# Four sample blocks at a time, the last product in two PSUM tiles, and a redrawn order of steps

## Chip, core and metric

The kernel runs on one core of a Trainium2 chip. The metric is the device time of one execution in microseconds (us). Engines are called as in the profile: PE (TensorE, matmuls; PEld its weight loads), DVE (VectorE), ACT (ScalarE), POOL (GpSimd), SP (SyncE, which here issues most DMA transfers).

## What is computed

The reference is one step of a decoder layer with D_MODEL 1024, for a prompt of 1024 tokens and a sample of 8 tokens. The parts that matter here are the last two:

```python
m = (jax.nn.sigmoid(g_a) * jnp.einsum('ble,ed->bld', y_a, w_pa)
     + jax.nn.sigmoid(g_b) * jnp.einsum('ble,ed->bld', y_b, w_pb))
h = h + _rmsnorm(jnp.einsum('bld,de->ble', m, w_out), post_g)
e = jnp.einsum('blp,pd->bld', p, w_ple)
gate = jax.nn.sigmoid(jnp.einsum('bld,de->ble', _rmsnorm(h, ple_in_g), w_pg))
h = h + _rmsnorm(gate * e, ple_out_g)
```

The product with `w_out` is called "output" below and the product with `w_pg` "gate". Ahead of them lie the combined input projection with its seven branches, the spatial gating, the pooling, and the products with `w_pa` and `w_pb`. All data are float32; products are formed from a high and a low part of each operand (three matmuls, high x high, high x low, low x high).

## The kernel before

**Products.** Each 1024 x 1024 product is made in four "pairs" of 256 rows or tokens, and each pair by Strassen's scheme: seven products P1 to P7 of half size in place of eight. One such product is one *step*: it prepares its weights, runs 12 matmuls of up to 512 columns into a PSUM tile, and has the tile evacuated by ACT or DVE. In output and gate the tokens are the stationary operand (`Turned`) and the rows are tokens (`Tokens`); PSUM tiles called `acct` come from three buffers. Output pairs 1 to 3 and all gate pairs go through `strassen_within` (line 757), whose tile `r2` takes P6, P5 and P3 one after the other by accumulation, with reads in between. In the trace the operand's name tells the product: `woB11`/`wgB11` is P1, `T2` P6, `T3` P7, `T1` P5, `B21` P2, `B22` P3, `T4` P4; a final h or l is the high or low part.

**The last gate pair** uses the order `LAST` (P1, P6, P7, P5, P2, P4, P3). Its last product, P3, is made in two column halves of 256 (`run_halves`, line 791), both in the one tile `r2`, and each half is handed to `user.direct`, which for the gate is `gated` (line 1586): a sigmoid on ACT out of PSUM, a product with the embedding on DVE, a sum of squares on ACT and a product with the gain on DVE. `gate_finish` then takes the root on POOL and writes the last rows of the result.

**The sample** (8 tokens) takes its output and gate rows from `sample_steps` (line 934). For both, eight blocks of 128 rows of the weights (`worow`, `wgrow`, 512 KB each) are loaded, and a *round* (`sample_round`, line 903) multiplies two blocks by the sample's 8 columns in four float32 matmuls that use four column groups of the array at once and accumulate in four parts of one bank, `sps`. Rounds are put between the steps of the prompt's products: loads after steps 0, 2, 4, 6 and rounds after steps 2, 4, 6, 8, counted from `OS` in output and `GS` in gate (line 36). After the last round `sample_sums` adds the four parts; output's sample then goes through `out_finish(S)` (norm, and a transfer on POOL's queue that adds `x_sample` to `hs`), `gate_norm(S)` and `gate_input(S)`.

**The order of the work** is not that of the source. A planner (`Planner`, line 95) collects all operations with estimated durations (`duration`), due times (`late`, worked back from PE's uses) and landing times of transfers (`lands`), then lets a simulated machine choose, on each engine, among what is ready. `LOAD` and `LEAD` say how long before its due time an operation may start, `PATIENCE` how long it may be passed over, and `HASTE` is the patience of the steps in `TURNS`. `TURNS` says after which step of output and gate (seven steps per pair, 0 to 27 output, 28 to 55 gate) the finish, the gate's norm and the turning of h for the gate are recorded for each pair of token blocks. The engines then run these orders as they stand, each in its own order. All operations are issued by one line, 369, which is why the profile names that line everywhere.

Of the kernel before, what the change touches and what calls it, by code (L numbers as in the profile page):

```python
# [11 lines left out]
AF = mybir.ActivationFunctionType  # L12
# [4 lines left out]
NB = D // P  # L17
# [3 lines left out]
HALF = 512  # L21
QUART = 256
# [2 lines left out]
QT = WIDE // 2  # L25
EPS = 1e-6
POOL_BUF = 15
FAST = (1, 1, 0, 1)
SIDES = (0, 1, 0, 1, 0, 0, 0, 0)
EARLY = 40.0  # L30
WE = 2
PUSH = {'norm': -5.0, 'half': 0.0, 'cut': 0.0, 'e': -4.0, 'we': -4.0, 'vw': -5.0, 'p': -1.0}
WARM = 8
HASTE = 8.0
TURNS = ((7, 8, 11), (14, 14, 18), (21, 26, 28), (30, 33, 35))
OS, GS = 5, 12
WINDOWS = (2, 4, 8, 16)
PLE = 256
SLOTS = 46
# [55 lines left out]
class Planner:  # L95
# [5 lines left out]

    SEEN = {"tensor": 0.25, "vector": 0.15, "scalar": 0.20, "gpsimd": 0.20}
    TABLES = {AF.Gelu_apprx_tanh: 1, AF.Sigmoid: 2, AF.Silu: 3}
    LOAD, LEAD, PATIENCE, RATE, SPARE = 14.98, 14.0, 55.8, 0.36, 3
    SPARED = 1.0

    def __init__(self, nc, slots, queues):
# [98 lines left out]
    def take(self, engine, method, args, kwargs):  # L206
        given = [*(("out" if i == 0 else "", a) for i, a in enumerate(args)), *kwargs.items()]
        writes = [a for k, a in given if k in ("out", "accum_out") and a is not None]
        reads = [a for k, a in given if k not in ("out", "accum_out") and hasattr(a, "tensor")]
        if kwargs.get("accum_op") is not None:  # L210
            reads += writes
        name = writes[0].tensor.name
        if engine == "tensor" and self.open is not None and self.open[0] == name:
            op = self.open[1]
        else:
            op = Op(engine, len(self.ops), self.clock, self.fixed)
            op.patience, op.push = self.patience, self.push
            self.ops.append(op)
        self.open = (name, op) if engine == "tensor" else None
        op.calls.append((method, args, kwargs))  # L220
        op.spent.append(op.busy)
        if method == "dma_start":
            run = min(self.run(a) for a in (writes[0], reads[0]))
            op.busy, op.moved = 1.0 if engine == "gpsimd" else 0.45, writes[0].size() * 4e-6 * (1 + 0.2 / run)
            op.lands = 2.0
            if kwargs.get("accum_op") is not None:
                op.moved, op.lands = 2 * op.moved, 3.5
        else:
            took = self.duration(engine, method, writes[0], reads, kwargs)
            op.busy += took  # L230
            if engine == "tensor" and not self.fixed:
                self.clock += took
            if engine == "scalar":
                op.table = self.TABLES.get(kwargs["func"], 0)
        for ap in reads:
            self.touch(op, ap, False)
        for ap in writes:
            self.touch(op, ap, True)
# [138 lines left out]
def hybrid_step(  # L377
# [7 lines left out]
    nc = tc.nc  # L385
# [6 lines left out]
    plan = Planner(nc, SLOTS, {"acc": 3, "bank": 2})  # L392
# [42 lines left out]
    def add(out, a, b):  # L435
        nc.vector.tensor_tensor(out=out, in0=a, in1=b, op=ALU.add)
# [17 lines left out]
    nc = plan  # L454
# [39 lines left out]
    class Operand:  # L494
# [37 lines left out]
        def at(self, what, k):  # L532
            return [part[:, k % 2, :] for part in self.parts[what, k // 2]]

    class Stored(Operand):


        ROWS = {"B11": ("b", 0, 0), "B21": ("b", 1, 0), "B22": ("b", 1, 1), "T2": ("low", 0, 0),
                "T1": ("low", 0, 1), "T4": ("high", 0, 0), "T3": ("high", 0, 1)}
# [71 lines left out]
    class Features:  # L611

        new = staticmethod(lambda: region("acc"))
# [16 lines left out]
    class Tokens:  # L630

        new = staticmethod(lambda: region("acct")[:, 0])
        view = staticmethod(lambda ps, wide: ps)
        pieces = staticmethod(lambda ps, wide: [(ps, slice(0, HALF))])
# [1 line left out]
        tail = False  # L636
        like = staticmethod(lambda t: t)

    def columns(c):

        class Part(Tokens):
            pieces = staticmethod(lambda ps, wide: [(ps[:, c], c)])
        return Part

    class Turned(Weights):

# [11 lines left out]
    def product(form, ps, weights, operand, what, first, last, again=False):  # L658

        plan.apart()  # L660
        wide = what not in ("B11", "B21", "T4")
        for k in range(4):
            if k == 2 and plan.clock < EARLY:
                plan.apart()
            (wh, wl), (xh, xl) = weights, operand.at(what, k)
            for i, (w, x) in enumerate(((wh, xh), (wh, xl), (wl, xh))):
                for o, c in form.pieces(ps, wide):
                    nc.tensor.matmul(o, w[:, k, :], x[:, c],
                                     start=first and k == 0 and i == 0, stop=last and k == 3 and i == 2,
                                     skip_group_check=again)  # L670
# [86 lines left out]
    def strassen_within(weights, operand, user, order=None):  # L757

        steps, at = [], {}
        plan = (("P1", "A11", "B11", "r1"), ("P6", "S2", "T2", "r2"), ("P7", "S3", "T3", "r3"),  # L760
                ("P5", "S1", "T1", "r2"), ("P2", "A12", "B21", "r1"), ("P3", "S4", "B22", "r2"),
                ("P4", "A22", "T4", "r3"))
        place = {p: r for p, _, _, r in plan}

        def evacuate(p):
            ps = at[place[p]]
            if p == "P1":
                both = slot("u", (P, 2, HALF))
                at["u"], at["w"] = both[:, 0], both[:, 1]
                nc.scalar.activation(out=at["w"], in_=ps, func=AF.Copy)  # L770
            elif p == "P6":
                add(ps, ps, at["w"])
                nc.scalar.activation(out=at["u"], in_=ps, func=AF.Copy)
            elif p == "P5":
                nc.scalar.activation(out=at["w"], in_=ps, func=AF.Copy)
                user.summed(1, 1, at["r3"], at["w"])
            elif p == "P2":
                user.direct(0, 0, ps)
            elif p == "P3":
                user.direct(0, 1, ps)  # L780
            elif p == "P4":
                user.summed(1, 0, ps, at["u"])

        for p, a, b, r in sorted(plan, key=lambda x: order.index(x[0])) if order else plan:
            def run(a=a, b=b, r=r):
                new = r not in at
                if new:
                    at[r] = Tokens.new()
                product(Tokens, at[r], weights.ready[a], operand, b, new, True, not new)

            def run_halves(a=a, b=b, r=r):
                for c in (slice(0, QUART), slice(QUART, HALF)):
                    product(columns(c), at[r], weights.ready[a], operand, b, False, True, True)
                    user.direct(0, 1, at[r][:, c], slice(HALF + c.start, HALF + c.stop))

            if order and p == order[-1]:
                steps.append(Step(lambda a=a: weights.prepare(a), run_halves, nothing))
            else:
                steps.append(Step(lambda a=a: weights.prepare(a), run, lambda p=p: evacuate(p)))
        steps[0].loads = lambda: (weights.fetch(), user.loads())  # L800
        steps[-1].after.append(user.finish)
        return steps

    class User:

        func = AF.Copy
# [93 lines left out]
                nc.tensor.matmul(ps, hi(k), wl, start=False, stop=False)  # L900
                nc.tensor.matmul(ps, lo(k), wh, start=False, stop=k == w.nk - 1)

    def sample_round(ps, turned, weights, r):

        plan.apart()
        for q in range(4):
            k, j = r + q // 2, q % 2
            nc.tensor.matmul(ps[32 * q : 32 * q + NS, :], turned[k], weights(k, j),
                             start=r == 0, stop=r == len(turned) - 2)
# [24 lines left out]
    def sample_steps(key, src, steps, turned, finish):  # L934
        rows, ps = {}, []

        def load(r):
            for k in (r, r + 1):
                t = rows[k] = slot(f"{key}row", (P, D))
                dma(t, src[k * P : (k + 1) * P, :])  # L940

        def run(r):
            if not ps:
                ps.append(bank("sps"))
            sample_round(ps[0], turned(), lambda k, j: rows[k][:, j * HALF : (j + 1) * HALF], r)
            if r == NB - 2:
                finish(ps[0])

        for i, r in enumerate(range(0, NB, 2)):
            at(steps[2 * i], lambda r=r: load(r))  # L950
            at(steps[2 * i + 2], lambda r=r: run(r))


    roots = {}
# [64 lines left out]
    turned = dram.tile([SEQ, D], F32, tag="vturned", name="vturned")  # L1019
# [9 lines left out]
    class V(User):  # L1029

        func = AF.Gelu_apprx_tanh
# [158 lines left out]
    class Gate(User):  # L1190
        func = AF.Sigmoid
# [7 lines left out]
    class U(User):  # L1199
        func = AF.Gelu_apprx_tanh  # L1200
# [4 lines left out]
    class ZA(User):  # L1205
        func = AF.Silu
# [84 lines left out]
    class ZB(User):  # L1291
        func = AF.Silu
# [102 lines left out]
    steps = [s for p in vsteps + gasteps for s in p] + every(usteps)  # L1395
# [8 lines left out]
    c = vsteps[0]  # L1404
# [471 lines left out]
```

## Time and profile before

| | us |
|---|---|
| median of 3 runs | 981.69 |
| the three runs | 981.69, 984.54, 978.53 |
| the profiled execution's own time | 979.92 |
| its span (first to last instruction) | 978.2 |
| PE busy in the span | 965.4 |
| DVE busy | 805.7 |
| ACT busy | 495.5 |

The profile belongs to one execution, and durations read from it are compared with that execution's own time; what lies between its span and its time (1.72 us) is before the first and after the last instruction. In a row of the timeline the columns are start and duration in us, engine, line, operation, output <- input, shapes, and count; a bracket at the end tells how long the engine had idled and what ended the idling. A row of the waits has total us, number of waits and the longest. A row of the table by stretches has the length, then busy time and instructions of PE, PEld, DVE, ACT and POOL (or of the one engine that was asked for), the granted clock of PE, the share of the DMA engines and GB/s.

### The profile page before, as it was taken

To read this page: it belongs to the slowest core of one execution; us is meant where nothing else is said; L and a number is where in the kernel's file an instruction comes from. 1 tells how busy PE (TensorE), PEld (TensorE's weight loads), DVE (VectorE), ACT (ScalarE), POOL (GpSimd) and SP (SyncE) were. 2 spreads that over 40 slices of the span, in tenths; PEclk is the share of its full clock that TensorE was granted. 3 is DMA by queue.
4 is the path that set the end of the run, shared out by engine and by line. 5 is a ranking of instruction groups with operands and counts; after the bars stand their busy time and mean duration, and the time that the engine had idled before them with its cause. 6 is when DMAs were issued, how large, how long until landed. Compare 5 with 4: busy or idle time off the path is not lost. (4 is left out here: it accounts for less than half of the span.)

```text
span 978.2 us, 15914 instructions
## 1 busy us (share of the span) xinstructions
PE 965.4 (99%) x6048; PEld 858.1 (88%) x6048; DVE 805.7 (82%) x1251; ACT 495.5 (51%) x847; POOL 72.8 (7%) x117
## 2 busy tenths in 40 slices
PE   9999999999999999999999999999999999999996
PEld 7889999999999998999999999999999997778775
DVE  7798568978879789887777897698699899779987
ACT  7674346767434544242423343463363273688655
POOL 2200000000000000000010100000000001323212
PEclk9999999999999999999999999999999999999998
DMA  9464654423457787541222266692592385698996
GB/s 347 148 151 88 152 135 148 162 95 116 171 213 275 257 281 238 188 153 54 87 76 93 75 218 244 222 376 91 170 370 87 120 306 177 160 300 296 222 326 209
DMA packets 128505, 185.81 MB, mean 190 GB/s; under 512 B 42150, under 2 KB 85198, under 8 KB 128421
## 3 DMA queue, kind: packets, MB, share of 16 engines
q1 hardware_dynamic: 126093, 176.91, 54.4%
q0 software_dynamic: 2048, 7.37, 4.2%
q8 instruction: 47, 0.77, 0.3%
q10 hardware_dynamic: 288, 0.52, 0.2%
q14 instruction: 29, 0.24, 0.1%
HBM read 129.27 MB, written 55.96 MB: 189 GB/s over the span
## 5 line engine op out<-in xcount | busy, mean ns | idle before, releaser
L369 DVE TENSOR_TENSOR u<-acc,u 128x520 f32<-128x520 f32 (+1 forms) x90 | 62.5, 695 | 29.8 <-PE acc L369 29.8
L369 POOL TENSOR_TENSOR rstd<-ms,mhalf 128x1 f32<-128x1 f32 (+1 forms) x37 | 30.1, 840 | 448.7 <-DVE ms L369 448.0
L369 ACT ACTIVATE u<-acc 128x512 f32<-128x512 f32 x39 | 23.2, 596 | 35.0 <-PE acc L369 32.5
L369 ACT ACTIVATE zbw<-zbs 128x512 fp32r<-128x512 f32 x16 | 10.0, 629 | 31.6 <-DVE zbs L369 25.8
L369 DVE TENSOR_TENSOR big<-big 128x1024 f32<-128x1024 f32 (+4 forms) x20 | 24.7, 1262 | 0.1
L369 POOL COPY big<-xb 128x1 f32<-128x1 f32 x8 | 3.5, 443 | 260.9 <-ACT xb L369 218.0
L369 ACT ACTIVATE big<-mix 128x256 f32<-128x256 f32 x32 | 11.9, 382 | 20.6 <-PE mix L369 19.7
L369 ACT ACTIVATE paw<-pas 128x512 fp32r<-128x512 f32 x16 | 10.1, 630 | 24.0 <-DVE pas L369 20.0
L369 ACT ACTIVATE pbw<-pbs 128x512 fp32r<-128x512 f32 x16 | 10.1, 630 | 22.3 <-DVE pbs L369 17.0
L369 PE MATMUL accm<-qh,wpoolw 128*128 128x260 f32 (+1 forms) x96 | 21.0, 320 | 0.0
L369 DVE TENSOR_TENSOR zbw<-zbs,zbw 128x512 fp32r<-128x512 f32 x16 | 10.9, 689 | 12.0 <-ACT zbw L369 11.9
L369 ACT ACTIVATE gbw<-gbs 128x512 fp32r<-128x512 f32 x16 | 10.1, 630 | 20.9 <-DVE gbs L369 11.7
L369 ACT ACT_TABLE_LOAD x11 | 14.1, 1283 | 7.4 <-PE acc L369 3.6
L369 ACT ACTIVATE junk<-h 128x512 bf16<-128x512 f32 x25 | 15.7, 627 | 3.5 <-DVE h L369 3.0
L369 DVE SCALAR_TENSOR_TENSOR zb<-accm,gvec,zb 128x512 f32<-128x512 f32 (+1 forms) x16 | 12.0, 750 | 6.5 <-PE accm L369 6.4
L369 PEld LDWEIGHTS accm<-qh,wpoolw 128*128 128x128 f32 x96 | 15.6, 189 | 1.9
L369 ACT ACTIVATE u<-acct 128x512 f32<-128x512 f32 x22 | 13.0, 590 | 7.4 <-PE acct L369 5.1
L369 DVE TENSOR_TENSOR paw<-pas,paw 128x512 fp32r<-128x512 f32 x16 | 10.9, 687 | 6.7 <-ACT paw L369 6.7
L369 ACT ACTIVATE mw<-ms 128x512 fp32r<-128x512 f32 x16 | 10.0, 625 | 12.4 <-DVE ms L369 9.7
L369 ACT ACTIVATE xbw<-xbs 128x512 fp32r<-128x512 f32 x16 | 10.0, 626 | 11.7 <-DVE xbs L369 10.0
L369 PE MATMUL mix<-wst,vh 128*128 128x256 f32 x64 | 15.6, 321 | 0.0
L369 ACT ACTIVATE uw<-us 128x512 fp32r<-128x512 f32 x16 | 10.0, 625 | 10.0 <-DVE us L369 5.9
(660 smaller groups left out, 3557.7 us busy)
## 6 DMA issues: line engine op xcount, KB each, us to landing
ga<-ga SPq DMA_DIRECT2D x16, 516.0 KB, 5.9
gb<-gb SPq DMA_DIRECT2D x16, 516.0 KB, 7.2
ya<-za SPq DMA_DIRECT2D x8, 516.0 KB, 4.9
yb<-zb SPq DMA_DIRECT2D x8, 516.0 KB, 2.6
x<-in_x_prompt_dram SPq DMA_DIRECT2D x8, 512.0 KB, 7.3
vraw<-in_w_in_dram SPq DMA_DIRECT2D x8, 512.0 KB, 5.9
e<-e SPq DMA_DIRECT2D x8, 512.0 KB, 5.9
vturned<-v SPq DMA_DIRECT2D x32, 128.0 KB, 3.4
```

Source lines behind the costliest of these rows:

```text
L369: getattr(getattr(self.nc, e), method)(*(self.real(a) for a in args), **{k: self.real(a) for k, a in kwargs.items()})
```

## The change

1. **Sample rows four at a time** (`ROWS = 4`). `sample_steps` loads four blocks at once and runs two rounds directly after each other; the second round isn't separated from the first in the planner (`apart=False`), so both are one piece of PE's order. The number of loads, matmuls and bytes is the same. Loads are recorded after steps 0 and 4 and rounds after steps 2 and 6 from `OS` and `GS`. `OS` goes from 5 to 3 and `GS` from 12 to 14, so output's rounds stand after steps 5 and 9 (before: 7, 9, 11, 13) and gate's after 16 and 20 (before: 14, 16, 18, 20). `out_finish(S)`, `gate_norm(S)` and `gate_input(S)`, which are placed relative to `OS`, move two steps forward.
2. **The last pair's `r2` in two tiles.** In the last gate pair, P6, P5 and P3 write the left 256 columns into an `acct` tile and the right 256 into a tile `acctb` from the two single banks. P6 and P5 become 24 matmuls of 256 columns each in place of 12 of 512; P6 is evacuated by two additions on DVE and two copies on ACT (before one and one), P5 by two copies (before one). P3 keeps its two halves, now each in its own tile.
3. **Steps drawn anew.** The planner's `LEAD` goes from 14.0 to 13.58, `PATIENCE` from 55.8 to 51.894, `HASTE` from 8.0 to 7.8; `TURNS` changes in its first two rows; an accumulating transfer of less than 0.3 MB is taken to land in 7.0 us, not 3.5 (this is the sample's alone). The order of all engines is worked out again from these.

```diff
+ROWS = 4
-HASTE = 8.0
-TURNS = ((7, 8, 11), (14, 14, 18), (21, 26, 28), (30, 33, 35))
-OS, GS = 5, 12
+HASTE = 7.8
+TURNS = ((7, 8, 8), (14, 17, 18), (21, 26, 28), (30, 33, 35))
+OS, GS = 3, 14
...
-    LOAD, LEAD, PATIENCE, RATE, SPARE = 14.98, 14.0, 55.8, 0.36, 3
+    LOAD, LEAD, PATIENCE, RATE, SPARE = 14.98, 13.58, 51.894, 0.36, 3
...
-                op.moved, op.lands = 2 * op.moved, 3.5
+                op.moved, op.lands = 2 * op.moved, 3.5 if op.moved > 0.3 else 7.0
...
+    class Pieces(Tokens):
+        pieces = staticmethod(lambda ps, wide: ps)
...
         def evacuate(p):
             ps = at[place[p]]
+            if order and p in ("P6", "P5"):
+                for o, c in ps:
+                    if p == "P6":
+                        add(o, o, at["w"][:, c])
+                    nc.scalar.activation(out=at["u" if p == "P6" else "w"][:, c], in_=o, func=AF.Copy)
+                if p == "P5":
+                    user.summed(1, 1, at["r3"], at["w"])
+                return
...
-                if new:
+                if new and order and r == "r2":
+                    two = Tokens.new(), bank("acctb")
+                    at[r] = [(t[:, :QUART], slice(i * QUART, (i + 1) * QUART)) for i, t in enumerate(two)]
+                elif new:
                     at[r] = Tokens.new()
+                if order and r == "r2":
+                    product(Pieces, at[r], weights.ready[a], operand, b, new, True, not new)
+                    return
                 product(Tokens, at[r], weights.ready[a], operand, b, new, True, not new)
 
             def run_halves(a=a, b=b, r=r):
-                for c in (slice(0, QUART), slice(QUART, HALF)):
-                    product(columns(c), at[r], weights.ready[a], operand, b, False, True, True)
-                    user.direct(0, 1, at[r][:, c], slice(HALF + c.start, HALF + c.stop))
+                for o, c in at[r]:
+                    product(Pieces, [(o, c)], weights.ready[a], operand, b, False, True, True)
+                    user.direct(0, 1, o, slice(HALF + c.start, HALF + c.stop))
...
-    def sample_round(ps, turned, weights, r):
+    def sample_round(ps, turned, weights, r, apart=True):
-        plan.apart()
+        if apart:
+            plan.apart()
...
         def load(r):
-            for k in (r, r + 1):
+            for k in range(r, r + ROWS):
...
-            sample_round(ps[0], turned(), lambda k, j: rows[k][:, j * HALF : (j + 1) * HALF], r)
-            if r == NB - 2:
+            at_once = turned()
+            for s in range(r, r + ROWS, 2):
+                sample_round(ps[0], at_once, lambda k, j: rows[k][:, j * HALF : (j + 1) * HALF], s, s == r)
+            if r == NB - ROWS:
                 finish(ps[0])
 
-        for i, r in enumerate(range(0, NB, 2)):
-            at(steps[2 * i], lambda r=r: load(r))
-            at(steps[2 * i + 2], lambda r=r: run(r))
+        for i, r in enumerate(range(0, NB, ROWS)):
+            at(steps[ROWS * i], lambda r=r: load(r))
+            at(steps[ROWS * i + 2], lambda r=r: run(r))
```

More of the change, by code (lines that the diff above doesn't have):

```diff
@@ L637, in hybrid_step @@
         like = staticmethod(lambda t: t)
[L639 to L643, printed above, removed]
+    class Pieces(Tokens):
+        pieces = staticmethod(lambda ps, wide: ps)
     class Turned(Weights):
```

## The prediction

> **What bounds the kernel now.** I read the page first, then the waits of TensorE (PE), then the timeline around each wait.
>
> ```profile
> span 978.2 us, 15914 instructions
> PE 965.4 (99%) x6048; PEld 858.1 (88%) x6048; DVE 805.7 (82%) x1251; ACT 495.5 (51%) x847; POOL 72.8 (7%) x117
> ```
>
> PE is busy 965.4 of 978.2 us. The change does not alter the amount of arithmetic, so it can gain only from the 12.8 us that PE idles, or from busy time in which PE does not stream at its pace. The waits give the idle time before PE's last instruction:
>
> ```profile
> PE warm L369 <- DVE heat L369: 1.5, 1, 1.5
> PE acct L369 <- ACT h L369: 1.2, 1, 1.2
> PE acc L369 <- DVE za L369: 0.7, 1, 0.7
> PE acct L369 <- ACT ge L369: 0.6, 1, 0.6
> PE e L369 <- DVE pl L369: 0.2, 1, 0.2
> ```
>
> That is 4.2 us; the other 8.6 us lie after PE's end. Two of the five rows touch code that the change edits: "ACT h" (in the output projection) and "ACT ge" (inside the last product). They carry the argument, beside the sample's rounds, where PE counts as busy but loses pace.
>
> **Sample's rounds.** The first gate round, with the matmuls on both sides, and then the same round's own matmuls in slices of 0.05 us:
>
> ```profile
> 927.70 0.40 PE L369 MATMUL acct<-wgB11h,hw 128*128 128x512 f32 x1
> 928.03 1.04 PE L369 MATMUL sps<-wgrow,sst 128*8 128x512 f32 x8
> 929.00 0.50 PE L369 MATMUL acct<-wgT2h,hw 128*128 128x512 f32 x1
> 929.34 0.40 PE L369 MATMUL acct<-wgT2l,hw 128*128 128x512 f32 x1
> ...
> 931.86 0.40 PE L369 MATMUL acct<-wgT3h,hw 128*128 128x512 f32 x1
> ...
> 934.43 0.40 PE L369 MATMUL acct<-wgT3h,hw 128*128 128x512 f32 x1
> ```
>
> ```profile
> 928.40:928.45 0.05, 0.05 (x4) 1.00 0.24 82
> 928.45:928.50 0.05, 0.05 (x8) 1.00 1.36 410
> ```
>
> An undisturbed product of 12 wide matmuls goes from 931.86 to 934.43, 11 steps of 0.234 us. From 927.70 to 929.34 there are 1.64 us for two such steps and one round, so a round costs 1.64 - 0.47 = 1.17 us. Its eight records run as two groups of four side by side: the second group starts just after 928.45, 0.44 us after the first. The streaming is therefore 2 x 0.44 = 0.88 us; the other 0.29 us are lost in entering and leaving (0.33 us ahead of the round, 0.34 behind its successor, 0.09 at its end). The change runs the eight rounds of output and gate as four pairs with nothing between the two of a pair. If the second round follows at the group's pace, each pair saves one 0.29: 4 x 0.29 = **-1.2 us**. No pair stands back to back in this trace, so the bounds are 0 (the second round costs 1.17 too) and 1.2 (it can't stream in under 0.88). I take 1.2, since within a round the second group already follows the first without a gap.
>
> The loads stay eight per matrix, now four at a time, and pass other transfers on SP's queue by up to two steps. The landing of the gate's eight rows (wgrow):
>
> ```profile
> DMA to landing us min/median/max: 6.3/6.7/11.5
> ```
>
> The planner lets a load start 14.98 us before it is due, so even 11.5 leaves 3 us; where that cover is gone, PE stands for the difference. I cost it at nothing. Four rows hold two more slots for a few steps; no wait for slots shows.
>
> **The stall at 864 us.** Here are ACT's queue, PE behind it, and the transfer ahead of it:
>
> ```profile
> 856.42 0.63 ACT L369 ACTIVATE mw<-ms 128x512 fp32r<-128x512 f32 x1 [4.30 <-DVE ms L369]
> ...
> 857.96 0.62 ACT L369 ACTIVATE junk<-h 128x512 bf16<-128x512 f32 x1
> ...
> 860.75 0.19 ACT L369 ACTIVATION_READ_ACCUMULATOR junk<-h 128x1 f32 x1
> 862.67 1.06 ACT L369 ACTIVATE hn<-hs 8x1024 f32<-8x1024 f32 x1 [1.73 <-DMA hs<-in_x_sample_dram]
> ...
> 864.51 0.60 ACT L369 ACTIVATE junk<-acct 128x512 bf16<-128x512 f32 x1
> ...
> 865.10 0.59 ACT L369 ACTIVATE h<-acct 128x512 f32<-128x512 f32 x1
> ```
>
> ```profile
> 858.86 0.40 PE L369 MATMUL acct<-woB22h,mw 128*128 128x512 f32 x1
> ...
> 864.17 0.39 PE L369 MATMUL acct<-woT4h,mw 128*128 128x512 f32 x1
> 865.74 0.50 PE L369 MATMUL acct<-woB11h,mw 128*128 128x512 f32 x1 [1.18 <-ACT h L369]
> ```
>
> ```profile
> hs<-in_x_sample_dram POOLq DMA_DIRECT2D x1, 32.0 KB, 6.3
> ```
>
> ACT works in order. It does the four squares of the prompt's gate norm (857.96 to 860.94), then stands 1.73 us at the sample's square, whose 32 KB accumulating transfer took 6.3 us to land. Behind it wait the square and copy that free an accumulator whose product had ended when B22 began at 858.86. The next pair's first product needs that buffer, and PE stands 1.18 us. The planner put the sample's square there because it assumed a landing of 3.5. The change makes that 7.0 for the small transfer alone, and starts the output's sample work at step 3, not 5: its last round runs after step 9 instead of 13, its finish and norm at 13 and 15 instead of 15 and 17. Two steps at 12 x 0.234 = 2.8 us each put the transfer 5.6 us earlier, against a wait of 1.73. Without the sample's piece (1.73 + 1.06) ahead of it, the copy ends by about 865.7 - 2.8 = 862.9, before PE asks for the buffer at 864.56. So **-1.2 us**, bounds 0 and 1.2; I take all of it. With the sample go two ACT squares, three PSUM reads, a store on SP, eight small transposes: the same instructions, elsewhere.
>
> What is late next? The turned steps move too. Pair 1's gate norm goes from step 14 to 17, yet its squares ran only at 857.96 (waiting for h), so they hardly move. Pair 0's gate input goes from 11 to 8: eight block loads on SP and two vector transposes, earlier. These are the places where a new wait could stand in ACT's queue.
>
> **The last product.** Timeline of the tail, all engines:
>
> ```profile
> 965.90 0.29 PE L369 MATMUL acct<-wgB22h,hw 128*128 128x256 f32 x1
> ...
> 967.57 0.28 PE L369 MATMUL acct<-wgB22h,hw 128*128 128x256 f32 x1
> 967.88 0.47 ACT L369 ACTIVATE ge<-acct,hscales 128x256 f32<-128x256 f32 x1 [0.33 <-PE acct L369]
> ...
> 968.41 0.38 PE L369 MATMUL acct<-wgB22h,hw 128*128 128x256 f32 x1 [0.56 <-ACT ge L369]
> ...
> 969.46 0.28 PE L369 MATMUL acct<-wgB22h,hw 128*128 128x256 f32 x1
> 969.59 0.68 DVE L369 TENSOR_TENSOR ge<-ge,out 128x512 f32<-128x512 f32 x1
> ...
> 969.78 0.47 ACT L369 ACTIVATE ge<-acct,hscales 128x256 f32<-128x256 f32 x1 [0.36 <-PE acct L369]
> ...
> 970.28 0.43 DVE L369 TENSOR_TENSOR ge<-eback,ge 128x256 f32<-128x256 f32 x1
> ```
>
> The first twelve matmuls are the left half, but three of the right run before ACT's read (fifteen start by 967.57, at 0.119 us). ACT's read waits for these three, and the other nine wait for ACT, since one tile holds both halves. With two tiles 24 matmuls run through: 965.90 + 23 x 0.119 + 0.28 = 968.92 instead of 969.46 + 0.28 = 969.74, so PE ends 0.82 us earlier. The span gets less: DVE is busy until 970.27 with the row at 969.59, and goes straight into the right half at 970.28. Only reordered work on DVE can pass more on. Bounds 0 and 0.82, and I take the middle rounded up, **-0.5 us**.
>
> The price is that two earlier products of that pair (P6 and P5) are written as pairs of 256 columns. The nearest rows are pairs of 260:
>
> ```profile
> 46.53 0.41 PE L369 MATMUL acc<-xB12h,vw 128*128 128x260 f32 x2
> ...
> 52.30 0.40 PE L369 MATMUL acc<-xB22h,vw 128*128 128x260 f32 x2
> ```
>
> 24 pairs in 5.77 us are 0.240 each, against 0.234 for one of 512 columns: 24 x 0.006 = **+0.1 us**, bounds 0 and 0.2. The Trainium skill (TensorEngine Tiling (Array Packing), Instruction Overhead) says that each matmul has about 60 cycles of overhead; with the 2.4 GHz that TensorE: Matmul & The Clock Gate (Specifications) names, 24 more instructions would by my estimate cost 24 x 25 ns = 0.6 us. The rows just quoted don't show such an addition, so I go by them.
>
> The evacuation of P6 becomes two adds and two copies; P5's becomes two copies. Their cover:
>
> ```profile
> 955.02 0.70 DVE L369 TENSOR_TENSOR acct<-acct,u 128x512 f32<-128x512 f32 x1
> ...
> 956.17 0.60 ACT L369 ACTIVATE u<-acct 128x512 f32<-128x512 f32 x1
> ...
> 957.58 0.39 PE L369 MATMUL acct<-wgT1h,hw 128*128 128x512 f32 x1
> ```
>
> P5 starts at 957.58 and needs the copy, which ended at 956.77: 0.8 us of slack. Two adds of 0.43 (as at 970.28) add 0.16 to DVE, two reads of 0.47 (as at 969.78) 0.34 to ACT: 0.5 together, hidden. Without the slack PE would wait that 0.5.
>
> **Sum.** -1.2 - 1.2 - 0.5 + 0.1 = -2.8 us. The profiled execution's own time is 979.92, 1.72 above its span, so it would become 977.1 with a span of 975.4. It lies 1.77 below the median of the three runs shown, 981.69; from that median the same sum gives **978.9 us**, my prediction.
>
> **Rivals.** (a) *The gain is given back to DVE.* From the table by stretches:
>
> ```profile
> 875.00:900.00 25.00, 25.00 (x110) 20.32 (x109) 24.89 (x34) 22.90 (x40) 7.22 (x3) 1.00 0.97 315
> ```
>
> DVE has 0.11 us free of 25 there, just behind the stall: a PE that arrives 1.8 us earlier (the stall and two pairs) may wait for its weights. That leaves -1.0: 980.7. Against it: PE does not wait there today, and weights are prepared up to three steps ahead. (b) *The merged rounds save nothing*, as their cost is streaming and weight loads: -1.6, 980.1. (c) *The two tiles don't part the halves*, because DVE's order binds the tail anyway: -2.3, 979.4. (d) *Slower:* the redrawn order puts the four squares (2.98 us) ahead of the copy that frees the accumulator at step 21, where today only the sample's pieces do the harm. The copy then ends up to 2.98 us later than today's 865.69 and the wait is up to 1.18 + 2.98 = 4.16 in place of 1.18; with the other terms, +3.0 - 1.2 - 0.5 + 0.1 = +1.4: 983.1. The mechanism begins to cost when that copy ends after 864.56, and outweighs the other gains of 1.6 us from a copy that ends about 1.6 us later than today's. For it: ACT's order there is the planner's, and patience, lead and haste all change. Against it: ACT has 4.3 us of idle time before 856.42. (e) *More:* the redrawn order also removes the wait for "DVE za" of 0.7 and the tail gains all 0.82, -3.8: 977.9.
>
> **How the numbers follow.** Forecast 0.50 (with c inside it, 0.08 of the 0.50), (a) 0.17, (b) 0.08, (d) 0.15, (e) 0.10. The cases run from 977.9 to 983.1. The three runs of before spread about 3 us to each side of their median, so the median of a new set can be off by some 2 to 3 in itself. Eight in ten is therefore 974.8 to 983.4. About 1% (9.8 us) is what a measurement of this kernel can tell from no change; no case reaches it. I leave 0.03 for a faster order than any row shows and 0.03 for a redrawn order with several new stalls, so 0.94 stays within 1%.
>
> **What would show it.** Right: four groups of 16 "sps" records in output and gate, each costing PE about 2.05 us and not 2.34; no wait of PE on "ACT h"; no wait of PE on "ACT ge" inside B22, with PE's last matmul 0.8 us closer to its first of that product; PE's waits in total about 2.4 us. Wrong: a new row above 1 us in PE's waits, above all on ACT or DVE between 860 and 930; a PE wait on the sample's rows; or a distance from PE's last matmul to the span's end that grows by as much as PE gains (today 978.2 - 969.74 = 8.46 us).

## The result

The changed kernel takes 988.62 us (median of 7 runs, 981.64 to 993.09) against 980.94 for the kernel before (7 runs, 978.53 to 984.54). The ratio is 1.0074, interval 1.0047 to 1.0100: **slower, by 7.7 us between the medians,** where I forecast 2.8 us faster, and outside the range of 974.8 to 983.4. It is still within the 1% that I had called "the same".

The page of the changed kernel, and its waits of PE (total us, number, longest):

```profile
span 991.4 us, 15974 instructions
PE 967.6 (98%) x6072; PEld 861.1 (87%) x6072; DVE 806.6 (81%) x1252; ACT 496.0 (50%) x849; POOL 64.3 (6%) x117
```

```profile
PE acct L370 <- DVE ge L370: 6.9, 1, 6.9
PE warm L370 <- DVE heat L370: 1.5, 1, 1.5
PE pp L370 <- DMA p<-in_p_prompt_dram: 1.5, 1, 1.5
PE acc L370 <- DVE za L370: 1.4, 1, 1.4
PE acct L370 <- ACT u L370: 1.3, 1, 1.3
```

Before, there was no wait of PE above 1.5 us; now one of 6.9 stands there. The wait on "ACT u" is new too; it stands at 896.20 us, in the gate's first pair. "ACT h" (1.2) and "ACT ge" (0.6), which the change was to remove, are gone. This execution's own time is 993.09, the longest of the seven and 4.5 above their median, and that of before lay 1 us below its own, so the two spans differ by 13.2 us where the medians differ by 7.7.

**Where the 13.2 us lie.** From the first matmul of each stage and the last of all in the two timelines: output's first matmul comes at 801.0 instead of 798.5 (+2.5, from waits near the start that change from run to run); output takes 85.5 instead of 87.6 (-2.1); from the gate's first matmul to PE's end 94.0 instead of 83.7 (+10.3); from PE's end to the span's end 10.9 instead of 8.46 (+2.4).

**The stall.** PE and then DVE in the timeline, around 933 to 945 us; the bracket is the idle time and what ended it:

```profile
932.67 0.40 PE L370 MATMUL acct<-wgT2h,hw 128*128 128x512 f32 x1
939.96 0.76 PE L370 MATMUL acct<-wgT3h,hw 128*128 128x512 f32 x1 [6.89 <-DVE ge L370]
940.52 0.63 PE L370 MATMUL acct<-wgT3l,hw 128*128 128x512 f32 x1
...
944.79 0.60 PE L370 MATMUL acct<-wgT3h,hw 128*128 128x512 f32 x1
```

```profile
930.55 0.21 DVE L370 TENSOR_SCALAR sofar<-ssq 128x1 f32<-128x1 f32 x2
937.39 1.25 DVE L370 STREAM_TRANSPOSE big<-hblocks 128x1024 f32<-128x1024 f32 x1 [6.63 <-DMA hblocks<-h]
938.56 0.65 DVE L370 TENSOR_TENSOR hw<-hs,hw 128x512 fp32r<-128x512 f32 x1
939.13 0.68 DVE L370 TENSOR_TENSOR ge<-acct,u 128x512 f32<-128x512 f32 x1
```

Read from the end: PE needs an `acct` buffer that DVE frees with ge<-acct,u at 939.13. DVE, in order, has been idle since 930.76 and stands 6.63 us at a transposition whose block of h has not landed. The chain of waits says how long that block took:

```profile
922.98 14.29 DMA hblocks<-h
...
937.39 1.25 DVE big L370
```

Over all 32 such loads, the changed kernel and then the one before:

```profile
DMA to landing us min/median/max: 2.4/4.8/14.3
```

```profile
DMA to landing us min/median/max: 2.9/3.9/10.1
```

SP's queue, first of the changed kernel, then of the kernel before, shows what went ahead:

```profile
915.77 0.43 SPq L370 DMA_DIRECT2D h<-h  x1
916.31 1.55 SPq L370 DMA_DIRECT2D wgrow<-wg  x2
917.96 0.40 SPq L370 DMA_DIRECT2D h<-h  x1
919.18 0.80 SPq L370 DMA_DIRECT2D wgrow<-wg  x2
921.60 1.81 SPq L370 DMA_DIRECT2D hblocks<-h  x4
```

```profile
914.66 1.34 SPq L369 DMA_DIRECT2D wgrow<-wg  x2
916.09 0.38 SPq L369 DMA_DIRECT2D h<-h  x1
916.56 3.04 SPq L369 DMA_DIRECT2D hblocks<-h  x4
920.03 1.67 SPq L369 DMA_DIRECT2D wgrow<-wg  x2
```

Before, two of the sample's 512 KB rows went ahead of block 7's four loads and two behind. Now all four, 2 MB, go ahead. In the trace's records of packets, the packets of 4 KB (rows and stores) fill the DMA engines at some 410 GB/s from 919.5 to 926.5 us, and the blocks' 512 packets of 1 KB begin only behind them; 480 are through by 930.

The last 32 run beside two accumulating transfers of POOL (`ge<-h`, issued at 924.35 and 927.77), whose 4 KB packets lie between 928.7 and 936.3 us and take 0.33 us each. From 930.87 on the blocks' packets come one at a time, mostly 0.36 us apart, and at the end one packet of POOL's lies between each two: it looks like one DMA engine that is behind and takes turns between two queues. The last comes at 936.9. DVE fell idle at 930.76, when 25 of the 512 were left, so its whole wait is this last part: the rows made the blocks late enough to fall under POOL's transfers. The second execution of the changed kernel (e1 below) shows the same 0.36 us. In the kernel before, the last of these packets came at 928.0 and the transposition began at 929.88; the loads had less than 2 us of cover.

The Trainium skill (DMA: Bandwidth & Descriptors, Queues, rings and completion order) says that each DMA engine consumes a ring's descriptors in order; the order of these packets agrees. It also says that an engine takes turns between the queues that it has work for, packet by packet; the 0.36 us, one packet of each queue, agree with such turns. The page counts 9 to 17 descriptors to a packet; here a turn is one packet as the profile records it, and the measurement decides. Why so many of the blocks' packets were left to the end is open.

**The clock.** The product behind the stall ran at 0.43 us a matmul instead of 0.23. In the table by stretches, the last three columns are the granted clock, the DMA share and GB/s:

```profile
925.00:930.00 5.00, 5.00 (x23) 4.05 (x22) 4.39 (x7) 3.34 (x7) 1.70 (x3) 1.00 1.10 282
930.00:940.00 10.00, 3.11 (x15) 2.21 (x13) 3.37 (x8) 2.30 (x7) 0.00 (x0) 0.75 0.46 91
940.00:945.00 5.00, 5.00 (x12) 3.72 (x12) 4.86 (x9) 3.23 (x7) 0.56 (x1) 0.50 0.73 222
945.00:950.00 5.00, 5.00 (x29) 2.69 (x29) 3.50 (x4) 0.63 (x1) 1.48 (x2) 0.98 0.84 231
```

Half the clock was granted from 940 to 945. The product took 5.4 us from its first matmul to the next instruction (939.96 to 945.32) instead of 12 x 0.234 = 2.8, so the stall cost 6.9 + 2.5. The Trainium skill (TensorE: Matmul & The Clock Gate, What's actually happening) puts the drop to half speed behind at least one idle window of about 3.4 us, and the return behind at least one such window of sustained work. The trace agrees with both: 6.9 us of idling, then about 5 us of work at half clock. The 1.2 us wait of before left the clock at 1.00 (from 860 to 885 us).

**What went as forecast.** A merged round, ACT at the sample's square, and the last product:

```profile
820.33 0.40 PE L370 MATMUL acct<-woT1h,mw 128*128 128x512 f32 x1
820.65 1.90 PE L370 MATMUL sps<-worow,big 128*8 128x512 f32 x16
...
822.83 0.39 PE L370 MATMUL acct<-woB22l,mw 128*128 128x512 f32 x1
```

```profile
854.07 1.04 ACT L370 ACTIVATE hn<-hs 8x1024 f32<-8x1024 f32 x1
```

```profile
977.50 0.28 PE L370 MATMUL acct<-wgB22h,hw 128*128 128x256 f32 x1
...
978.92 0.28 PE L370 MATMUL acctb<-wgB22h,hw 128*128 128x256 f32 x1
...
980.23 0.28 PE L370 MATMUL acctb<-wgB22h,hw 128*128 128x256 f32 x1
```

A pair of rounds costs 822.83 - 820.33 - 0.47 = 2.03 us (forecast 2.05; 2.34 before). The sample's square has no bracket, so it waits for nothing. The last product runs 24 matmuls in 3.0 us without a wait (3.84 before).

### The profile page after: what moved, and what is told of

It is laid out like the page before. It is cut to its first block, busy times and chain, and to the rows that moved or that the text cites. A ratio compares the mean times of both kernels' runs of the same rounds, so it can differ in the third digit from the quotient of the medians.

```text
span 991.4 us, 15974 instructions
## 1 busy us (share of the span) xinstructions
PE 967.6 (98%) x6072; PEld 861.1 (87%) x6072; DVE 806.6 (81%) x1252; ACT 496.0 (50%) x849; POOL 64.3 (6%) x117
## 4 chain that ended last, share of the span: by engine, by line
PE 80%; DMA 9%; DVE 6%; issue 2%; ACT 1%; SPq 1%; POOL 0%; DVEq 0%; ACTq 0%; POOLq 0%
PE acc L370 65%; PE acct L370 8%; DMA hblocks<-h 3%; PE accm L370 2%; PE e L370 2%; DMA wgraw<-in_w_pg_dram 1%; DMA eback<-e 1%; PE mix L370 1%; DVE ge L370 1%; SPq L370 1%; DVE big L370 1%; DMA woraw<-in_w_out_dram 1%; PE pst L370 1%; DMA weraw<-in_w_ple_dram 1%; PE sps L370 1%
## 5 line engine op out<-in xcount | busy, mean ns | idle before, releaser
L370 ACT ACTIVATE zbw<-zbs 128x512 fp32r<-128x512 f32 x16 | 10.1, 629 | 38.1 <-DVE zbs L370 17.1
L370 ACT ACTIVATE pbw<-pbs 128x512 fp32r<-128x512 f32 x16 | 10.1, 631 | 26.0 <-DVE pbs L370 19.1
L370 ACT ACTIVATE gbw<-gbs 128x512 fp32r<-128x512 f32 x16 | 10.1, 630 | 20.7 <-DVE gbs L370 14.4
L370 PE MATMUL acct<-wgT3h,hw 128*128 128x512 f32 x32 | 12.5, 455 | 6.9 <-DVE ge L370 6.9
L370 DVE STREAM_TRANSPOSE big<-hblocks 128x1024 f32<-128x1024 f32 x8 | 9.9, 1238 | 9.8 <-DMA hblocks<-h 9.8
L370 ACT ACTIVATE u<-acct 128x512 f32<-128x512 f32 (+1 forms) x22 | 12.5, 570 | 10.3 <-PE acct L370 5.3
L370 ACT ACTIVATE gbw<-gbraw 128x512 fp32r<-128x512 f32 x12 | 7.4, 628 | 17.9 <-DMA gbraw<-in_w_in_dram 10.8
L370 ACT ACTIVATE hw<-hs 128x512 fp32r<-128x512 f32 x16 | 9.9, 624 | 12.6 <-DVE big L370 7.1
```

The costliest lines, as they stand in the source:

```text
L370: getattr(getattr(self.nc, e), method)(*(self.real(a) for a in args), **{k: self.real(a) for k, a in kwargs.items()})
```

## The experiments

All time ratios are against the kernel before, run on the same chip beside the variant, with their 95% intervals. The stage columns come from each kernel's profiled execution, counted from output's first matmul, which takes out the 4 us by which the start varies; DVE's end is that of its last operation on the results (`ge`).

| kernel | median us | ratio | gate's start | PE's end | DVE's end | span's end |
|---|---|---|---|---|---|---|
| before | | | 87.6 | 171.3 | 175.9 | 179.7 |
| before, run as a variant (e14) | 980.19 | 1.0006 (0.9994 to 1.0018) | 87.4 | 172.2 | 176.8 | 180.6 |
| after | 988.62 | 1.0074 (1.0047 to 1.0100) | 85.5 | 179.5 | 186.5 | 190.4 |
| after again (e1) | 989.07 | 1.0072 (1.0046 to 1.0097) | 85.5 | 178.0 | 184.5 | 188.5 |
| four rows behind the blocks (e2) | 983.41 | 1.0022 (1.0007 to 1.0037) | 85.5 | 172.1 | 179.2 | 182.9 |
| two rows behind the blocks (e5) | 982.98 | 1.0022 (1.0007 to 1.0037) | 85.5 | 170.1 | 177.2 | 181.1 |
| before, blocks behind the rows (e3) | 986.49 | 1.0057 (1.0035 to 1.0078) | 88.9 | 176.9 | 181.5 | 185.4 |
| redrawn only (e4) | 983.59 | 1.0020 (1.0006 to 1.0034) | 86.1 | 170.7 | 176.9 | 182.0 |
| gate rows only (e6) | 982.09 | 1.0012 (0.9994 to 1.0030) | 86.9 | 169.9 | 175.1 | 180.2 |
| tiles only (e7) | 982.73 | 1.0023 (1.0006 to 1.0041) | 87.6 | 170.5 | 176.4 | 181.5 |
| output rows, landing, tiles (e8) | 982.84 | 1.0013 (0.9997 to 1.0029) | 87.4 | 173.8 | 179.2 | 183.8 |
| output rows only (e15) | 981.52 | 1.0016 (1.0005 to 1.0028) | 86.2 | 172.2 | 176.9 | 180.6 |
| before, less PE work (e13) | 981.08 | 1.0001 (0.9988 to 1.0015) | 87.5 | 172.1 | 177.0 | 180.9 |
| before, less DVE work (e9) | 980.23 | 1.0002 (0.9983 to 1.0020) | 87.5 | 171.2 | 175.7 | 179.8 |
| tiles only, less DVE work (e10) | 980.90 | 1.0006 (0.9989 to 1.0023) | 87.7 | 170.6 | 175.7 | 180.8 |
| e5, less DVE work (e11) | 981.53 | 1.0012 (0.9995 to 1.0030) | 85.5 | 169.7 | 174.8 | 179.9 |
| tiles only, store earlier (e12) | 982.26 | 1.0013 (0.9997 to 1.0030) | 87.9 | 170.8 | 176.7 | 181.6 |

### Is it the order on SP's queue?

The changed kernel once more, without an edit.

> The changed kernel once more, on the chip of the next three, for comparison. Both theories: 986 to 990 us, about 1.007 of before, with a wait of PE on DVE of several us in the third gate pair and a halved clock behind it.

It repeats: ratio 1.0072, with PE waiting 6.3 us for DVE and DVE 6.2 at most for a block. Next, the changed kernel with the four loads of gate rows put behind block 7's loads on SP's queue; every other queue as it was.

```python
rows, blocks = loads("wgrow"), loads("hblocks")    # positions in the drawn order
first, last = rows[:4], blocks[6 * 4 + 3]          # play `first` right behind `last`
```

> The changed kernel with one edit to SP's order: the first four wgrow loads (2 MB) are issued behind the four block loads of token block 7, not ahead of them; every other engine's order is the same. Theory A (the rows ahead of the blocks on SP's queue make the blocks land late, and DVE stands at their transpose with the accumulators' evacuation behind it): the wait of DVE on these blocks falls from 6.6 to under 2 us, PE's wait on DVE in that pair goes, the clock stays at full speed, and the time falls by 8 to 10 us to 978 to 980, 0.997 of before. Theory B (the blocks land late because POOL's accumulating transfers run beside them, whatever SP's order): the waits stay and the time is 986 to 990.

The time falls by 5.7 us (989.07 to 983.41), less than the 8 to 10 expected. PE no longer waits for DVE's addition, DVE's longest wait for a block is 2.5 us, and PE waits 1.0 us for the rows instead, which are now late. The blocks' 1 KB packets are through at 924.8, before POOL's packets begin at 926:

```profile
PE acc L382 <- DVE za L382: 1.3, 1, 1.3
PE sps L382 <- DMA wgrow<-wg: 1.0, 1, 1.0
PE acct L382 <- ACT u L382: 1.0, 1, 1.0
```

With `first = rows[2:4]`, so only the second pair behind, as in the kernel before:

> The changed kernel with only the second pair of wgrow loads issued behind block 7's loads: two rows (1 MB) ahead of the blocks, as in the kernel before. With all four behind, PE waited 1.0 us on a row. Theory A with the dose (the wait grows with the bytes ahead of the blocks): DVE waits under 2.5 us on blocks, no wait on rows, 981 to 983 us, at or up to 1 us under the version with four behind. Rival (the order of the two matters, not the bytes): as the changed kernel, 986 to 990.

No wait for the rows is left either; the median is 982.98, and the blocks' packets are again through at 924.9, ahead of POOL's. The other way round, the kernel *before* with block 7's loads put behind the second pair of rows (`first, last = blocks[6 * 4 : 7 * 4], rows[3]`):

> The kernel before with one edit to SP's order, the reverse of the other: the four block loads of token block 7 are issued behind the second pair of wgrow loads, as in the changed kernel. Theory A: DVE waits 3 to 7 us on the blocks, PE stands 2 to 7 us, and the time rises to 984 to 990. Theory B: no change, 980 to 982.

It loses 5.6 us (ratio 1.0057) with nothing else changed. Its largest waits of PE, and SP's queue:

```profile
PE acct L381 <- DVE hw L381: 2.5, 1, 2.5
PE acct L381 <- ACT h L381: 2.5, 1, 2.5
```

```profile
919.18 4.97 SPq L381 DMA_DIRECT2D wgrow<-wg  x2
924.20 3.04 SPq L381 DMA_DIRECT2D hblocks<-h  x4
```

Taking the order away and putting it in thus show about the same size: **the order of these two groups of transfers is worth about 5 to 6 us of the 7.7** (5.6 to 5.7 by the medians, 4.9 to 5.6 by the ratios). The way is not the same in e3. There SP stood at the second of the two rows until DVE had transposed an earlier block (923.81), so block 7's loads were issued some 7 us later than in the kernel before, and then landed in at most 8.6 us. DVE waited 3.1 us for them. The landing was no longer than before (10.1), so what made them late was the standing queue and not the bytes ahead. Nor was it tried to move POOL's transfers, so their part in the 6.6 us of the changed kernel is read from its trace and not tested.

### The parts one at a time

The redrawn order alone (new LEAD, PATIENCE, HASTE, TURNS and landing time; rows two at a time, one tile), as an edit of the changed kernel:

```diff
-OS, GS = 3, 14
+OS, GS = 5, 12
...
-    sample_steps("wo", ..., out_sample)               # and the same for "wg"
+    sample_steps("wo", ..., out_sample, 2)
...
-            if order and p in ("P6", "P5"):           # and the other branches for the tiles
+            if False:
```

> Before with the third part of the change alone: the planner's LEAD, PATIENCE, HASTE, the two rows of TURNS and the 7.0 us landing; sample's rows two at a time with OS and GS as before, one PSUM tile for the last product. Its SP order also has four wgrow loads ahead of block 7's loads. Theory A1 (the redraw alone brings the late blocks): 985 to 989 us with the same wait of PE on DVE. Theory A2 (the four rows at a time bring it, since they also take more slots and are loaded in one piece): 979 to 981, no such wait.

It costs 2.0 us (1.0020) and reproduces neither the whole loss nor none; its SP queue too has four rows ahead of block 7's loads, but in the profiled execution the longest wait for a block was 2.0 us. It does not tell what the order is worth in it: between the rows and block 7's loads SP stood 12.0 us for DVE's `hs`, and the loads were issued at 928.36, when the rows had landed. The three single edits on the kernel before:

```diff
-    sample_steps("wg", ..., embed_gate_sample)        # e6, with GS = 14
+    sample_steps("wg", ..., embed_gate_sample, 4)
```

> Before with four rows at a time in the gate alone (GS 14, ROWS 4 there; output, planner's numbers and PSUM tiles as before). SP's order keeps two rows ahead of block 7. Theory A: two merged rounds save 0.6 us and nothing else moves: 980 to 981, 0.999 of before. Rival (four rows at a time by themselves delay the blocks or the embedding's loads): 983 to 988.

For e7 only the diff's lines on `Pieces`, `evacuate`, `new and order` and `run_halves` are put in (part 2 of the change); for e8 these and

```diff
-OS, GS = 5, 12
+OS, GS = 3, 12
...
-                op.moved, op.lands = 2 * op.moved, 3.5
+                op.moved, op.lands = 2 * op.moved, 3.5 if op.moved > 0.3 else 7.0
...
-    sample_steps("wo", ..., out_sample)
+    sample_steps("wo", ..., out_sample, 4)
```

> Before with the two PSUM tiles alone. Prediction's term: PE's end 0.8 us earlier, the span 0.4 shorter: 980.5. Rival (DVE binds the tail): PE's end 0.8 us earlier and the distance from it to the span's end 0.8 us longer, 980.9 as before.

> The parts that the traces speak for, without the redrawn numbers: before with four rows at a time in output (OS 3), the 7.0 us landing and the two tiles; gate's rows two at a time, LEAD, PATIENCE, HASTE and TURNS as before. SP's order has two rows ahead of block 7. Theory A: two merged rounds (-0.6), the stall at 864 us (-1.2) and the tiles (0 to -0.4): 978.7 to 979.2, 0.998 of before. Rival (whatever is gained ahead of the gate is given back there, since transfers and DVE set its pace): 980.5 to 982.

None gains, and each median lies outside the times that either of its theories gave. In e6 and e7 PE ends 1.4 and 0.7 us earlier than in before (two runs of the unchanged kernel differ by 0.9). PE's end to the span's end is 10.3 us in e6 and 11.0 in e7 instead of 8.46. In e7 DVE's last operations read:

```profile
971.34 0.21 DVE L370 TENSOR_SCALAR ms<-ssq,sofar 128x1 f32<-128x1 f32 x1
971.47 0.41 DVE L370 TENSOR_TENSOR ge<-ge,out 128x256 f32<-128x256 f32 x1
971.80 2.73 DVE L370 SCALAR_TENSOR_TENSOR ge<-ge,rstd,hback 128x512 f32<-128x512 f32 x4
```

All four final scalings stand behind the last statistics; the kernel before has three there, and DVE ended at 974.35 in before and 974.53 in e7. The 0.7 us that PE won is not there at DVE's end.

### Who sets the end?

Three explanations were left: DVE's load, the stores, or a comparison that is unfair to any variant. For less DVE work the seven multiplications by the output gain on DVE (4.2 us between 962 and 972) are left out; the last rows lack that factor.

```python
def gain(c):                             # c is (engine, (method, args, keywords))
    ...                                  # vector tensor_tensor, out is a `ge`, in1 is `out`
return [c for c in todo if not gain(c)]
```

> The kernel before, without the seven multiplications by the output gain on DVE (ge<-ge,out, TENSOR_TENSOR) of blocks 6 and 7 and of the sample: its last rows then lack that factor. In the profile of before they take 0.67 us five times and 0.42 us twice between 961.8 and 972.4 us, 4.2 us in all. Theory 1 (in the last 20 us DVE is bound as closely as PE is, so that in before both end together): PE's end stays at 969.7, and DVE, which is not late any more, ends some 4.0 to 4.6 us behind it, 973.5 to 974.3: time 0.1 to 1 us below before. Theory 2 (PE alone sets the end): the two 128x256 and one 128x512 multiplications behind the last product are all that counts, and DVE's end moves with PE's in this kernel and the next one alike: 0.4 to 1.1 us below before here.

> The kernel before with only the last product in two PSUM tiles (as in the run of the tiles alone: PE's end at 968.65, DVE's at 974.53, span 979.6), without the same seven multiplications. Theory 1 (DVE's queue took what the tiles gave): with the 4.2 us of DVE gone, DVE's end follows PE's: 968.6 + 4.0 to 4.6 = 972.6 to 973.3, 1.2 to 1.9 us earlier than with the tiles alone, and 0.7 to 1.1 us earlier than the kernel before that was lightened in the same way. Theory 2 (the tiles' 1.1 us were lost to something else than DVE, such as the store or a slower clock): DVE ends within 0.5 us of 974, no earlier than in the lightened kernel before.

> The changed kernel with the second pair of gate rows behind block 7's loads (PE's end at 967.92, DVE's at 975.03, span 978.9 in its profile, median 982.98), without the same seven multiplications. Theory 1 (PE has gained what was forecast, and DVE keeps it): DVE's end falls to 967.9 + 4.0 to 4.6 = 971.9 to 972.5, 2.5 to 3.1 us earlier, span near 976.3, and the time lies 1.5 to 2.5 us below the lightened kernel before. Theory 2 (the gain is lost elsewhere, by a lower clock or by other stalls in most executions): it stays at or above the lightened kernel before.

Theory 1 holds for e9, where nothing changes (1.0002; counted from output's start, DVE's end is 175.7 after 175.9 and 176.8). For e10 and e11 it asked for too much: DVE ended at 974.07 and 973.69, not at 972.6 and 971.9. With DVE's load gone, the rest of the chain behind the last product stays serial: ACT's three squares, the root on POOL, four scalings. Against e9, DVE's end gains nothing in e10 and 0.8 us in e11, and the medians gain nothing: here PE's end was brought forward and DVE's work cut at once, and the time did not fall.

```python
late, first = stores(1024)[-1], stores(512)[0]      # positions of the stores, by columns
return [*todo[:first], todo[late], *todo[first:late], *todo[late + 1:]]
```

> The kernel before with only the last product in two PSUM tiles, and the last store of a whole block (512 KB, out_dram<-ge 128x1024) put ahead of the four half stores in SP's queue, where before has it; with the tiles alone it stands last but one. Theory 1 (the 512 KB take DMA time between the last results and the end): from DVE's end to the span's end 3.8 to 3.9 us as in before instead of 5.1 us, span 978.4, median 1.2 us below that of the tiles alone (982.73), so 981.5. Theory 2 (the length of that stretch is chance from execution to execution): 5.1 us again or anything between, and no shift of the median.

Theory 1 failed: 4.9 us from DVE's end to the span's end, not 3.8. The packets did change places, but then those of the four half stores came that much later. The place of the 512 KB store isn't the cause. Nor is it chance (theory 2): this stretch is 4.9 to 5.2 us in e4, e6, e7, e10, e11 and e12, 4.6 in e8 and 3.7 to 4.1 in all the others. What sets it stays open. Then PE alone: eight of the last pair's matmuls are left out of the kernel before, so two products lack their low part.

```python
low = [... "wgT1l", "wgB21l" ...][-8:]   # none of them starts or ends an accumulation
return [c for i, c in enumerate(todo) if i not in low]
```

> The kernel before, without 8 of the last gate pair's 128x512 matmuls (those with the low halves wgT1l and wgB21l, so two of its products lack that part): at 0.23 us each PE's end moves 1.86 us forward, from 969.74 to 967.9, with DVE's, ACT's and SP's orders unchanged. Theory 1 (in the last 15 us DVE and ACT set the end as much as PE, and what PE gains there is not the kernel's): DVE's end moves by less than half of that, to 973.4 to 974.3; time 0 to 0.9 us below before. Theory 2 (PE sets the end): DVE's end moves with PE's, to 972.5, and the time falls by 1.9 us.

The clearest run of the study: 1.86 us of PE's work is gone (6040 matmuls instead of 6048), and the time does not fall: ratio 1.0001, with an interval from -1.2 to +1.5 us that leaves out the 1.9 us of theory 2 (by the medians it is 1.35 us longer). In its waits of PE

```profile
PE acct L376 <- ACT u L376: 1.6, 2, 1.2
PE acct L376 <- ACT ge L376: 1.6, 1, 1.6
PE acct L376 <- DVE sofar L376: 0.5, 1, 0.5
```

"ACT ge" has grown from 0.6 to 1.6 and "DVE sofar" is new, and even PE's end stays where it was in e14 (172.1 and 172.2). Theory 1 is shown for the last pair: PE waits there for what DVE and ACT hand on.

> The kernel before, unchanged, run as a variant. If the comparison is even: ratio 1.000, within 0.0015. If it favours the kernel before: 1.001 to 1.003, as the variants with other orders show, and then their excess is no property of theirs.

The comparison is even within its interval (1.0006). An excess of 1.0012 or 1.0013, as in e6, e8, e11 and e12, can't be told from that; 1.0016 to 1.0023 (e2, e4, e5, e7, e15) lies only a little above. In this profile of the unchanged kernel PE has no wait on "ACT h" at 864 us; one of 1.06 us stands at 874.41 instead, on ACT's `u`.

Last, output's rows alone:

```diff
-OS, GS = 5, 12
+OS, GS = 3, 12
...
-    sample_steps("wo", ..., out_sample)
+    sample_steps("wo", ..., out_sample, 4)
```

> The kernel before with the output stage's rows of w_out loaded and multiplied four at a time, and nothing else changed (the planner then draws the later queues anew around it). Theory 1 (a gain of PE in the output stage is kept only if DVE and ACT get earlier too): the two merged rounds show 2.03 us each instead of 2.34, PE reaches the gate 0.6 us earlier, and the end moves by 0 to 0.6 us: time 980 to 981. Theory 2 (any new drawing of the queues costs 1 to 3 us at the end): 981.5 to 983.5, with PE's end to span's end 10 to 11 us.

Output alone gained 1.4 of the 1.8 us forecast for it, 87.6 to 86.2 us, part of it from the "ACT h" wait, which went away too. The gate gave it back: 86.0 us instead of 83.7 and 84.7 in the two runs of the unchanged kernel, with new waits of PE of 0.48, 0.26 and 0.69 us on DVE's `hw` and ACT's `u` between 892 and 920; PE's end is 172.2 against 171.3 and 172.2. In e8, with the same rows, output itself gained nothing (87.4): "ACT h" is gone, and waits of 0.65 and 0.55 us on ACT's `u` stand at 873.81 and 880.15.

## Why the prediction was wrong

- **The rounds: right.** 2.03 us a pair, forecast 2.05.
- **The stall at 864 us: right as a mechanism.** The sample's square waits for nothing, and the stall is gone. Output took 2.1 us less; the forecast had 0.6 (two pairs) + 1.2. That its removal is worth 1.2 us is not shown: in e14, e8 and the changed kernel waits on ACT's `u` stand 10 to 30 us later.
- **The last product: right for PE, wrong for the span.** PE needs 3.0 us as worked out, 0.82 less. The -0.5 for the span should have been 0, the lower bound and rival (c): DVE's end did not get earlier in e7. The price of the pairs was near its forecast: P6 and P5 took 5.79 us for 24 pairs (2.94 and 2.85 us to the next product), 0.17 above 24 x 0.234.
- **"I cost it at nothing": the step that failed.** I looked whether the *rows* would land in time (they did: PE does not wait for them in the changed kernel) and not at what the rows pass. "Pass other transfers on SP's queue by up to two steps" was the loss itself: block 7's loads got 2 MB put ahead of them and landed after 14.3 us, in place of at most 10.1 for any block before, with less than 2 us of cover. "What is late next?" named pair 0's block loads, which were not the ones. Of the total, about 5 to 6 us come from this order (e2, e5; e3 the other way round).
- **A long wait has a second price.** No term and no rival had the half clock: 2.5 us on top of 6.9 in the profiled execution.
- **The sum as such.** Even without the stall nothing of the 2.8 us is left (e5: +2 us, not -2.8). I added up PE's time because PE is busy 99%, but from 875 to 905 us DVE is as full. In the table by stretches, first the kernel before, then the changed one:

```profile
885.00:905.00 20.00, 20.00 (x88) 16.25 (x87) 19.72 (x31) 16.50 (x29) 9.12 (x4) 1.00 0.83 296
```

```profile
885.00:905.00 20.00, 18.71 (x82) 14.93 (x81) 19.96 (x28) 17.00 (x32) 5.28 (x2) 1.00 0.83 309
```

  DVE was busy 19.72 of 20 us and is busy 19.96 in the changed kernel, where PE now stands 1.29 us (the "ACT u" row, at 896.20; 1.0 to 1.4 us in e1, e2 and e5 too). The chain of waits behind it runs from 879 to 892 us almost wholly through DVE's work on weights and h. Of the 2.1 us that output gained, this wait takes 1.3. Rival (a), "given back to DVE", with 0.17, was right as a mechanism and too small: I let it take only the 1.8 us ahead of 875 us, and e13 shows that a gain in the last pair isn't kept either, there by waits on ACT's `ge` and DVE's `sofar`.
- **Rival (d)** had the form (an in-order queue that holds an accumulator's evacuation) and 983.1, but the wrong engine, place and size. The test that I named for "wrong" was the right one: a new row above 1 us, and PE's end to span's end grown from 8.46 to 10.9.

**Open.** Why e5, without the stall, still lies 0.7 to 3.6 us above before (its PE ends at 170.1, earlier than in both runs of the unchanged kernel, its DVE at 177.2, later than in both); how much of it is the redrawn DVE order and how much the measurement is not separated. Nor was it tried to move DVE's and ACT's work together, so no kernel here beats the one before.

## What to carry over

When a load moves forward in an in-order queue, cost every transfer that it passes: how much later that one starts (2 MB ahead at the 410 GB/s seen here are some 5 us), which transfers of other queues it then falls under, how much cover it had, and who stands in order behind it. Where two engines are both nearly full in a stage, don't count a gain on one as the kernel's; leaving out a little work on one engine (as in e13) tells this in a single run. That cutting both brings a gain is not shown: e10 and e11 bring PE's end forward and cut DVE's work, and gained nothing. Price a stall of several microseconds with the product behind it at half speed.

## What was not expected of the hardware

Half the clock for about 5 us after 6.9 us of idling (0.43 us instead of 0.23 a matmul), while a wait of 1.2 us left none. Four loads of 128 KB took 14.3 us behind 2 MB on their queue, and the last 25 of their 512 packets trailed by some 6 us, mostly 0.36 us apart, while accumulating transfers on POOL's queue were under way with packets of 0.33 us each.
